# Gates before the convolved projections in an SSD and GLA layer, and decay triangles scaled four heads at a time

## The chip, the core and the metric

The kernel runs on one core of a Trainium2 chip. The metric is the device time of one execution in microseconds. The core's engines each run their own instruction queue and wait for one another by semaphores: TensorE (PE, matrix products; PEld is its weight load), VectorE (DVE), ScalarE (ACT), GpSimd (POOL) and SyncE (SP, here only the issue of weight transfers).

## The reference

The reference runs two blocks over 256 tokens of width 1024 and 256 context tokens. The first block has two layers, and the change lies in the second of them, "layer 1". Its mixer concatenates an SSD part and a GLA part, both scanned in both directions over the context and then the tokens. The modulation vectors (shift, scale and gate of the two norms) are products of the conditioning with a large matrix. Cut to what matters:

```python
z, xbc, dt_f, dt_b = split(p)                 # SSD
xbc = silu(dwconv_centred(xbc, conv_w, conv_b))
xs, bm, cm = split(xbc)                       # 512 + 256 + 256 channels
# scan in chunks of 128: decay = exp(segment sums of la), for 8 heads and both directions
y = rmsnorm((yf + yb + xs * d_skip) * silu(z)) # per group
# GLA: q, k, v, gate g; decayed scan in chunks, 4 heads
o = rmsnorm(scan(q, k, v)) * silu(g)
out = concat(y, o) @ w_out
```

Everything is computed in 32-bit precision.

## The kernel before

Weights arrive in tiles of 128x1024 numbers (512 KB) through SyncE's queue, strictly in the order in which the code asks for them, into a ring of four buffers (tile `w`, L32). A projection of 128 output channels, `gemm`, uses one tile: in halves of 512 columns it is split into a high part (ScalarE cast, L45) and a low part (VectorE subtraction, L46), and each of eight blocks is multiplied in three passes (L223, L224, L225) with the activations, whose parts are named `h0h`, `h0l` to `h7h`, `h7l`. One segment of activations is 256 columns. A projection of the tokens alone is therefore 24 matmuls, one of context and tokens is 48.

In `layer1` the small projections, q, k and v come first. Then the generator `gla` (L1007 on) is started: per chunk it makes decays, the intra-chunk products by levels (L1055 to L1081, L1078 being the last level's product for a chunk) and the states (L1099 to L1112); its last part makes the outputs from states and intra-chunk weights (L1132, L1133), their inverse norms on ScalarE (L186 and L195, after the sums of L209) and scales by them (L1135). The code then asks for the eight convolved projections xs, bm and cm: a copy out of PSUM (ScalarE L849), one tap on ScalarE (L851) and four multiply-adds on VectorE (L853), then silu by a tanh (L1213) and a VectorE operation (L1215). Inside the loop, behind projection 0, stand all the modulation steps that remain, two groups of 16 weight tiles; a group multiplies each tile with four matmuls (L154), copies and transposes the result (L161). After the convs ScalarE loads another table of functions (L177; logarithm and exponential), the rest of `gla` is taken, and then come the eight projections of the gates: z of SSD and gs of GLA, four each, halved into SBUF by L1233.

`ssd` (L906 on) follows: transposes of xs and bm (L918, L930) into the tile `sc`, products with the step sizes (L924, L927, `xd` and `xw`), a copy `bt` (L932), the chunk states (L936). For each of two chunks, two directions and two groups of four heads, the mask `TRI` is scaled by each head's log decay (L975, tile `lt`), multiplied by two constant matrices (L978, L980), put through the exponential (L981, L982; tiles `MT` and `CE`), and multiplied by the scores on GpSimd (L983) and by cm on VectorE (L984); the outputs are L992, L993 and L995. Then comes the output projection `w_out`, half of which needs only GLA's outputs (`o4` to `o7`) and is free to run earlier, and the memory stage (L1244 on).

The order of instructions on an engine is chosen by a scheduler from its own costs when the kernel is built, within the dependencies, and is fixed at run time. So an engine that waits for its next instruction runs none of the later ones.

Of the kernel before, what the change touches and what calls it, by code (L numbers as in the profile page):

```python
# [14 lines left out]
ALU = mybir.AluOpType  # L15
AX = mybir.AxisListType
PSUM = bass.MemoryType.PSUM
P = 128
# [58 lines left out]
class Kern:  # L77
# [827 lines left out]
    def ssd(self, pool, xs, bm, cm, z, d4, la, wend, etot, c1, out):  # L905
        nc = self.nc  # L906
# [52 lines left out]
        for c in range(2):  # L959
            ps = self.psum("sc")  # L960
            for gr in range(2):
                nc.tensor.matmul(ps[:, 128 * gr : 128 * gr + 128], lhsT=bm[gr][:, 256 + 128 * c : 384 + 128 * c],
                                 rhs=cm[gr][:, 128 * c : 128 * c + 128], start=True, stop=True)
            pair = []
            for d in range(2):
                cb = g("cb", (P, 2, 128), 2)
                nc.vector.tensor_tensor(cb, ps[:, 0:256].rearrange("p (g i) -> p g i", g=2),
                                        TRI[d].unsqueeze(1).broadcast_to([P, 2, 128]), op=ALU.mult)
                MT, CE = g("MT", (P, 8, 128), 2), g("CE", (P, 8, 128), 2)
                pair.append((MT, CE))  # L970
                for gr in range(2):
                    hs = slice(4 * gr, 4 * gr + 4)
                    lt = g("lt", (P, 4, 128), 2)
                    for h in range(4):
                        nc.vector.tensor_scalar(lt[:, h, :], TRI[d], la[:, 2 + c, 8 * d + 4 * gr + h : 8 * d + 4 * gr + h + 1], None, op0=ALU.mult)  # L975
                    l2 = lt.rearrange("p h i -> p (h i)")
                    p1 = self.psum("sc")
                    nc.tensor.matmul(p1, lhsT=ST[d], rhs=l2, start=True, stop=True)  # L978
                    p2 = self.psum("sc")
                    nc.tensor.matmul(p2, lhsT=self.C("ones"), rhs=l2, start=True, stop=True)  # L980
                    nc.scalar.activation(MT[:, hs, :], p1.rearrange("p (h i) -> p h i", h=4), AF.Exp)  # L981
                    nc.scalar.activation(CE[:, hs, :], p2.rearrange("p (h i) -> p h i", h=4), AF.Exp)  # L982
                    nc.gpsimd.tensor_tensor(MT[:, hs, :], MT[:, hs, :], cb[:, gr, :].unsqueeze(1).broadcast_to([P, 4, 128]), op=ALU.mult)  # L983
                    nc.vector.tensor_tensor(CE[:, hs, :], CE[:, hs, :],  # L984
                                            cm[gr][:, 128 * c : 128 * c + 128].unsqueeze(1).broadcast_to([P, 4, 128]), op=ALU.mult)
            for q in range(4):
                po = self.psum("po")
                for h in range(2):
                    o = po[64 * h : 64 * h + 64, 0:128]
                    hh = 2 * q + h  # L990
                    for d in range(2):
                        nc.tensor.matmul(o, lhsT=xd[d][c][:, hh, :], rhs=pair[d][0][:, hh, :], start=(d == 0), stop=False)  # L992
                        nc.tensor.matmul(o, lhsT=H[d][c][:, hh, :], rhs=pair[d][1][:, hh, :], start=False, stop=(d == 1))  # L993
                cs = slice(128 * c, 128 * c + 128)
                nc.vector.scalar_tensor_tensor(yt[q][:, cs], xs[q][:, 256 + 128 * c : 384 + 128 * c], self.V("d_skip")[:, q : q + 1], po[:, 0:128],  # L995
                                               op0=ALU.mult, op1=ALU.add)
# [140 lines left out]
    def layer1(self, xc, xl, sm, hm, HL):  # L1137
# [78 lines left out]
            return i  # L1216

        tanh, mods = [], (x for i in (1, 2) for x in self.mod_steps(1, i, cp, "mm"))
        for i in range(8):
            t = (xs + bm + cm)[i]  # L1220
            self.conv(cp, self.gemm(st, 72 + 8 * i, *(h if i < 6 else h[1:])), i, t, cw, cb)
            if i == 0:
                for _ in mods:
                    pass
            tanh.append(silu(t, last))
        for _ in mods:
            pass
        self.table(tanh)
        for _ in gla:
            pass  # L1230
        last = self.last
        for i in range(8):
            nc.scalar.mul((z + gs)[i], self.gemm(st, 136 + 8 * i, h[1]), 0.5)  # L1233
        M.close()
        G.close()
        H.close()
# [430 lines left out]
def blocks(w):  # L1667

    w = np.asarray(w)
    k, n = w.shape  # L1670
    return w.reshape(k // P, P, n // P, P).transpose(1, 2, 0, 3).reshape(P, -1, P)


def wide(w):

    w = np.asarray(w)
    return w.reshape(-1, P, w.shape[1]).transpose(1, 0, 2).reshape(P, -1, P)


def stream(*parts):  # L1680
    s = np.concatenate(parts, axis=1).reshape(P, -1)
    assert s.shape[1] % 2048 == 0, s.shape
    return np.ascontiguousarray(s.reshape(P, -1, 2048).transpose(1, 0, 2))
# [16 lines left out]
def prep(inp):  # L1700
# [46 lines left out]
    for l in range(2):  # L1747
# [7 lines left out]
    small = np.zeros((1024, P), np.float32)  # L1755
    small[:, 0:16], small[:, 32:48] = C[:, 1536:], D[:, 1536:]
    xbc = C[:, 512:1536]
    d["w_in1"] = stream(blocks(small), blocks(D[:, 256:512]), blocks(D[:, 0:256]), wide(D[:, 512:1024]), blocks(xbc), blocks(C[:, :512]),
                        blocks(D[:, 1024:1536]), np.zeros((P, 8, P), np.float32))
    up = np.zeros((P, 512), np.float32)  # L1760
    up[32:48, :256], up[32:48, 256:] = f["l1_gk_up_f"], f["l1_gk_up_b"]
    d["gk_up"] = up
# [59 lines left out]
```

## Time and profile before

| | us |
|---|---|
| median of 3 runs | 2034.68 (2032.78 to 2048.92) |
| profiled execution | 2034.45 |
| its span | 2032.7 |
| PE busy | 1910.7 (94%) |
| DVE busy | 1415.6 (70%) |
| ACT busy | 1160.0 (57%) |
| POOL busy | 277.4 (14%) |

The mean granted clock of TensorE is 0.974 of full speed. The part of layer 1 that the change touches lies between about 990 and 1190 us. The profile gives, by time, the busy share of each engine in a stretch, the chain of work that ended last, and each instruction with its start, length and the idle time before it. L12 is line 12 of the kernel; a tile is named out<-in.

### The profile page before, as it was taken

The numbers are of one execution on the slowest core, as the hardware profiler recorded it, in microseconds if no ns is written. First come the engines' busy times: TensorE is split into PE (matmuls) and PEld (weight loads), VectorE is DVE, ScalarE is ACT, GpSimd is POOL, SyncE is SP. The second block draws the span as 40 slices with busy tenths as digits, with TensorE's granted clock in tenths as the row PEclk, the third lists the DMA queues.
The fourth block names the chain that finished last, engine by engine and source line by source line (L and its number), as shares of the span: only waits on it lengthen the run. The fifth ranks groups of instructions, "written<-read, shape, count | busy, mean of one in ns | idle before, by whom it ended". The sixth has DMA issues, their size and how long they took to land.

```text
span 2032.7 us, 42311 instructions
## 1 busy us (share of the span) xinstructions
PE 1910.7 (94%) x16330; PEld 1725.6 (85%) x16330; DVE 1415.6 (70%) x2962; ACT 1160.0 (57%) x2527; POOL 277.4 (14%) x407
## 2 busy tenths in 40 slices
PE   5999999889999999999979999999999999989997
PEld 2886678669889998899739789999889998889997
DVE  3775966579767685567588977567776656677664
ACT  3655653465545675566546668476565555465553
POOL 1521110230100000001230210000012201012210
PEclk8999999889999999999989999999999999999999
DMA  8542430625116565765376435666325554325553
GB/s 307 167 138 70 166 125 22 218 85 157 42 45 190 185 195 185 237 216 175 115 243 187 135 115 178 187 186 189 103 86 184 182 183 137 103 84 165 183 183 114
DMA packets 91785, 313.26 MB, mean 154 GB/s; under 512 B 10304, under 2 KB 17728, under 8 KB 91584
## 3 DMA queue, kind: packets, MB, share of 16 engines
q1 hardware_dynamic: 83376, 299.94, 46.2%
q10 hardware_dynamic: 8208, 10.63, 1.7%
q8 instruction: 128, 2.10, 0.4%
q14 instruction: 73, 0.60, 0.1%
HBM read 309.48 MB, written 1.05 MB: 153 GB/s over the span
## 4 chain that ended last, share of the span: by engine, by line
PE 75%; DVE 10%; DMA 5%; ACT 4%; issue 2%; POOL 2%; POOLq 0%; ACTq 0%; SPq 0%; DVEq 0%
PE mm L224 16%; PE mm L223 16%; PE mm L225 16%; PE po L224 3%; PE po L225 3%; PE po L223 3%; DMA w<-in_mod 2%; PE mm L154 2%; DVE lo L46 1%; PE sc L532 1%; PE po L1383 1%; DMA w<-in_w_in 1%; DMA w<-in_mlp 1%; ACT hi L45 1%; DVE yy L1539 1%
## 5 line engine op out<-in xcount | busy, mean ns | idle before, releaser
L46 DVE TENSOR_TENSOR lo<-w,hi 128x512 fp32r<-128x512 f32 x948 | 651.5, 694 | 277.8 <-ACT hi L45 258.4
L45 ACT CAST hi<-w 128x512 fp32r<-128x512 f32 x948 | 576.5, 618 | 424.7 <-PE mm L224 290.0
L223 PE MATMUL mm<-u_h,hi 128*128 128x256 f32 x1120 | 318.9, 285 | 5.1 <-ACT u_h L216 5.0
L224 PE MATMUL mm<-u_l,hi 128*128 128x256 f32 x1120 | 317.2, 283 | 0.6 <-DVE u_l L217 0.4
L225 PE MATMUL mm<-u_h,lo 128*128 128x256 f32 x1120 | 317.6, 284 | 0.0
L223 PEld LDWEIGHTS mm<-u_h,hi 128*128 128x128 f32 x1120 | 214.0, 191 | 8.0 <-ACT u_h L216 5.6
L224 PEld LDWEIGHTS mm<-u_l,hi 128*128 128x128 f32 x1120 | 214.4, 192 | 1.2 <-DVE u_l L217 1.2
L225 PEld LDWEIGHTS mm<-u_h,lo 128*128 128x128 f32 x1120 | 214.0, 191 | 0.1
L154 PE MATMUL mm<-w,cs 128*32 128x256 f32 x640 | 68.1, 451 | 30.2 <-DMA w<-in_mod 29.9
L1588 POOL TENSOR_TENSOR ut<-ut,gt 128x256 f32<-128x256 f32 x44 | 53.9, 1226 | 200.1 <-ACT hi L45 170.5
L256 POOL TENSOR_SCALAR hf<-hf,g,mT 128x256 f32<-128x256 f32 x24 | 18.7, 781 | 413.5 <-ACT h1h L255 311.3
L154 PEld LDWEIGHTS mm<-w,cs 128*32 128x32 f32 x640 | 18.7, 118 | 58.1 <-DMA w<-in_mod 33.4
L217 DVE TENSOR_TENSOR u_l<-relu,u_h 128x256 fp32r<-128x256 f32 x96 | 40.7, 425 | 28.2 <-ACT u_h L216 28.0
L347 POOL TENSOR_SCALAR sht<-shf,mu 128x256 f32<-128x256 f32 x28 | 38.2, 1365 | 106.5 <-ACT shf L345 106.5
L216 ACT CAST u_h<-ut 128x256 fp32r<-128x256 f32 x44 | 17.9, 406 | 57.9 <-POOL ut L1588 57.9
L217 DVE TENSOR_TENSOR u_l<-ut,u_h 128x256 fp32r<-128x256 f32 x44 | 18.7, 425 | 43.8 <-ACT u_h L216 43.8
L223 PE MATMUL mm<-h0h,hi 128*128 128x256 f32 x130 | 39.7, 309 | 7.2 <-ACT shf L345 3.6
L1540 POOL TENSOR_TENSOR xl<-xl,yy 128x256 f32<-128x256 f32 x16 | 14.2, 888 | 228.1 <-DVE yy L1539 228.1
L69 POOL TENSOR_TENSOR sq<-sq 128x256 f32<-128x256 f32 x24 | 21.1, 880 | 154.6 <-ACT sq L61 151.7
L824 ACT ACTIVATE relu<-relu 128x256 f32<-128x256 f32 x96 | 39.6, 416 | 3.8 <-DVE h7l L257 1.5
L225 PE MATMUL mm<-h0h,lo 128*128 128x256 f32 x130 | 38.6, 297 | 3.1 <-DVE lo L46 3.1
L216 ACT CAST u_h<-relu 128x256 fp32r<-128x256 f32 x96 | 38.6, 405 | 2.2
(1125 smaller groups left out, 6116.1 us busy)
## 6 DMA issues: line engine op xcount, KB each, us to landing
w<-in_mlp SPq DMA_DIRECT2D x192, 512.0 KB, 4.3
w<-in_w_in SPq DMA_DIRECT2D x102, 512.0 KB, 4.3
w<-in_mod SPq DMA_DIRECT2D x96, 512.0 KB, 5.4
w<-in_ffn_in SPq DMA_DIRECT2D x88, 512.0 KB, 3.9
w<-in_ffn_out SPq DMA_DIRECT2D x44, 512.0 KB, 4.5
w<-in_w_out SPq DMA_DIRECT2D x40, 512.0 KB, 3.8
w<-in_memkv SPq DMA_DIRECT2D x8, 512.0 KB, 3.9
xc<-in_ctxT ACTq DMA_DIRECT2D x16, 128.0 KB, 4.8
```

The source lines that it names most:

```text
L45: nc.scalar.copy(self.hi, w)
L46: nc.vector.tensor_tensor(self.lo, w, self.hi, op=ALU.subtract)
L69: self.eng.tensor_tensor(sq, sq, self.acc, op=ALU.add)
L154: nc.tensor.matmul(ps[32 * j : 32 * j + 32, o : o + 256], lhsT=self.cs[:, k, :], rhs=w[:, 256 * j : 256 * j + 256], start=(k == 0), stop=( ...
L216: nc.scalar.copy(hi, src)
L217: nc.vector.tensor_tensor(lo, src, hi, op=ALU.subtract)
L223: nc.tensor.matmul(out, lhsT=wh, rhs=xh, start=start, stop=False)
L224: nc.tensor.matmul(out, lhsT=wh, rhs=xl, start=False, stop=False)
L225: nc.tensor.matmul(out, lhsT=wl, rhs=xh, start=False, stop=stop)
L347: nc.gpsimd.tensor_scalar(t, f[:, 1:257], self.mu1[:, i : i + 1], None, op0=ALU.mult)
L824: nc.scalar.activation(r, r, AF.Square)
L1588: nc.gpsimd.tensor_tensor(w, w, t, op=ALU.mult)
```

## The change

Three edits. The loop of the gates stands ahead of the convolved projections and takes two modulation steps (four tiles of modulation weights) behind each projection; what modulation is left is taken behind that loop. The columns of the weight matrix are laid out in the new order on the host. In `ssd` the four scalings of a 128x128 mask become one multiplication of 128x512, with the mask and the decays broadcast.

```diff
--- before.py
+++ after.py
@@ -971,8 +971,8 @@
                 for gr in range(2):
                     hs = slice(4 * gr, 4 * gr + 4)
                     lt = g("lt", (P, 4, 128), 2)
-                    for h in range(4):
-                        nc.vector.tensor_scalar(lt[:, h, :], TRI[d], la[:, 2 + c, 8 * d + 4 * gr + h : 8 * d + 4 * gr + h + 1], None, op0=ALU.mult)
+                    nc.vector.tensor_tensor(lt, TRI[d].unsqueeze(1).broadcast_to([P, 4, 128]),
+                                            la[:, 2 + c, 8 * d + 4 * gr : 8 * d + 4 * gr + 4].unsqueeze(2).broadcast_to([P, 4, 128]), op=ALU.mult)
                     l2 = lt.rearrange("p h i -> p (h i)")
                     p1 = self.psum("sc")
                     nc.tensor.matmul(p1, lhsT=ST[d], rhs=l2, start=True, stop=True)
@@ -1216,21 +1216,21 @@
             return i
 
         tanh, mods = [], (x for i in (1, 2) for x in self.mod_steps(1, i, cp, "mm"))
+
+        for i in range(8):
+            nc.scalar.mul((z + gs)[i], self.gemm(st, 72 + 8 * i, h[1]), 0.5)
+            next(mods)
+            next(mods)
+        for _ in mods:
+            pass
         for i in range(8):
             t = (xs + bm + cm)[i]
-            self.conv(cp, self.gemm(st, 72 + 8 * i, *(h if i < 6 else h[1:])), i, t, cw, cb)
-            if i == 0:
-                for _ in mods:
-                    pass
+            self.conv(cp, self.gemm(st, 136 + 8 * i, *(h if i < 6 else h[1:])), i, t, cw, cb)
             tanh.append(silu(t, last))
-        for _ in mods:
-            pass
         self.table(tanh)
         for _ in gla:
             pass
         last = self.last
-        for i in range(8):
-            nc.scalar.mul((z + gs)[i], self.gemm(st, 136 + 8 * i, h[1]), 0.5)
         M.close()
         G.close()
         H.close()
@@ -1755,8 +1755,8 @@
     small = np.zeros((1024, P), np.float32)
     small[:, 0:16], small[:, 32:48] = C[:, 1536:], D[:, 1536:]
     xbc = C[:, 512:1536]
-    d["w_in1"] = stream(blocks(small), blocks(D[:, 256:512]), blocks(D[:, 0:256]), wide(D[:, 512:1024]), blocks(xbc), blocks(C[:, :512]),
-                        blocks(D[:, 1024:1536]), np.zeros((P, 8, P), np.float32))
+    d["w_in1"] = stream(blocks(small), blocks(D[:, 256:512]), blocks(D[:, 0:256]), wide(D[:, 512:1024]), blocks(C[:, :512]),
+                        blocks(D[:, 1024:1536]), blocks(xbc), np.zeros((P, 8, P), np.float32))
     up = np.zeros((P, 512), np.float32)
     up[32:48, :256], up[32:48, 256:] = f["l1_gk_up_f"], f["l1_gk_up_b"]
     d["gk_up"] = up
```

On TensorE the place of the last L1078 shows the first move. Before, modulation matmuls and GLA's outputs (L1132, L1133) follow the last L1078:

```order
L1078 MATMUL po<-ql_12502,kl_12503 64x64 x4
L154 MATMUL mm<-w,cs 32x256 x7
L1132 MATMUL po<-qe_12562,S_12725 128x128
L1132 MATMUL po<-qe_12563,S_12943 128x128
L1133 MATMUL po<-at_12474,v 128x128
L1132 MATMUL po<-qe_12562,S_12747 128x128
L1132 MATMUL po<-qe_12563,S_12921 128x128
L154 MATMUL mm<-w,cs 32x256 x4
```

Now a gate's matmuls end in front of it and a block of 16 modulation matmuls stands right behind:

```order
L1078 MATMUL po<-ql_12502,kl_12503 64x64
L224 MATMUL mm<-h7l,hi 128x256
L225 MATMUL mm<-h7h,lo 128x256
L154 MATMUL mm<-w,cs 32x256 x16
L1132 MATMUL po<-qe_12562,S_12725 128x128
L1132 MATMUL po<-qe_12563,S_12943 128x128
L1133 MATMUL po<-at_12474,v 128x128
L1132 MATMUL po<-qe_12562,S_12747 128x128
```

What moved: ahead of this point stood 109 modulation matmuls and the 48 of conv 0; now 64 and 118 matmuls of gates. 64 modulation matmuls and three gates stand behind.

On VectorE, the end of the convs before SSD: `cm` is the last convolved tile, `xc` are GLA's outputs being scaled, `lo` the low part of a weight half. Before:

```order
L1135 SCALAR_TENSOR_TENSOR xc_4418<-po,c_vecs,rstd 128x256
L46 TENSOR_TENSOR lo<-w,hi 128x512 x2
L1135 SCALAR_TENSOR_TENSOR xc_4419<-po,c_vecs,rstd 128x256
L46 TENSOR_TENSOR lo<-w,hi 128x512
L1135 SCALAR_TENSOR_TENSOR xc_4420<-po,c_vecs,rstd 128x256
L46 TENSOR_TENSOR lo<-w,hi 128x512
L1135 SCALAR_TENSOR_TENSOR xc_4421<-po,c_vecs,rstd 128x256
L975 TENSOR_SCALAR lt<-c_cst_9116,la 128x128 x8
L1215 SCALAR_TENSOR_TENSOR z_9126<-th,z_9126 128x256
```

And now:

```order
L1215 SCALAR_TENSOR_TENSOR cm_9125<-th,cm_9125 128x256
L1135 SCALAR_TENSOR_TENSOR xc_4418<-po,c_vecs,rstd 128x256
L1135 SCALAR_TENSOR_TENSOR xc_4419<-po,c_vecs,rstd 128x256
L1135 SCALAR_TENSOR_TENSOR xc_4420<-po,c_vecs,rstd 128x256
L1135 SCALAR_TENSOR_TENSOR xc_4421<-po,c_vecs,rstd 128x256
L927 TENSOR_TENSOR xw<-sc,wend 128x512 x2
L974 TENSOR_TENSOR lt<-c_cst_9116,la 128x512 x2
L1215 SCALAR_TENSOR_TENSOR z_9126<-th,z_9126 128x256
```

What moved: the low parts of the gates' weights between the scalings have gone, the first eight lt scalings became two operations, and SSD's first xw products stand ahead of them.

On TensorE at the start of SSD (`o4h` and so on are GLA's outputs in the output projection). Before, the matmuls in front of the transposes L918 are the last gate's:

```order
L225 MATMUL mm<-h7h,lo 128x256
L918 MATMUL sc<-c_cst_87,xs_9118 128x128
L918 MATMUL sc<-c_cst_87,xs_9119 128x128
L918 MATMUL sc<-c_cst_87,xs_9120 128x128
L918 MATMUL sc<-c_cst_87,xs_9121 128x128
L930 MATMUL sc<-c_cst_87,bm_9122 128x128
L930 MATMUL sc<-c_cst_87,bm_9123 128x128
L223 MATMUL mm<-o4h,hi 128x256
L224 MATMUL mm<-o4l,hi 128x256
L225 MATMUL mm<-o4h,lo 128x256
```

And now they are those of the last conv, with the last two sums for GLA's norms (L209) between:

```order
L225 MATMUL mm<-h7h,lo 128x256
L209 MATMUL sc<-sq,c_cst_87 128x256 x2
L918 MATMUL sc<-c_cst_87,xs_9118 128x128
L918 MATMUL sc<-c_cst_87,xs_9119 128x128
L918 MATMUL sc<-c_cst_87,xs_9120 128x128
L918 MATMUL sc<-c_cst_87,xs_9121 128x128
L930 MATMUL sc<-c_cst_87,bm_9122 128x128
L930 MATMUL sc<-c_cst_87,bm_9123 128x128
L936 MATMUL sc<-xw,bt 128x256 x4
```

What moved: the last L209 stand between the convs and SSD, and the output projection's matmuls are no longer between SSD's transposes and its states. Between the first L918 and SSD's own L209, 59 of the 96 matmuls of GLA's half of the output projection stood before, and 9 stand now.

## Rows read from the trace of the kernel before

**Rows 1.** stretches of the span, busy us (instructions) by engine, granted clock, DMA.

```profile
core 0: us, PE busy (x) PEld busy (x) DVE busy (x) ACT busy (x) POOL busy (x), PEclk, DMA share, GB/s
...
993.00:1074.00 81.00, 67.99 (x867) 37.44 (x865) 69.20 (x162) 45.15 (x131) 26.87 (x48) 0.89 0.61 208
...
1065.20:1137.00 71.80, 71.71 (x587) 66.59 (x585) 61.47 (x119) 50.14 (x102) 2.26 (x12) 1.00 0.62 193
...
1137.00:1184.00 47.00, 40.70 (x265) 28.02 (x265) 42.23 (x86) 24.11 (x48) 17.91 (x15) 1.00 0.20 62
```

**Rows 2.** TensorE's instructions from 993 to 1065.3, grouped; last column idle time before.

```profile
L154 PE MATMUL mm<-w,cs 128*32 128x256 f32 x222 | 25.4, 429 | 9.6 <-DMA w<-in_mod 9.5
```

**Rows 3.** the chain of waits: start us, length us, engine, tile, line.

```profile
1064.78 0.44 PE po L1078 x8
...
1072.20 0.57 PE mm L154 x8
...
1073.40 0.64 PE po L1132 x4
...
1076.11 0.42 PE po L1133 x2
...
1117.79 1.28 ACT L177
...
1139.50 1.12 PE sc L936 x4
```

**Rows 4.** VectorE in order: start us, us, engine, line, operation, out<-in.

```profile
1022.50 0.74 DVE L853 SCALAR_TENSOR_TENSOR xs<-cvf,conv_w,xs 128x512 f32<-128x512 f32 x1
...
1074.97 1.28 DVE L46 TENSOR_TENSOR lo<-w,hi 128x512 fp32r<-128x512 f32 x2
```

**Rows 5.** DMA issues from 990 to 1215: count, KB each, us to landing.

```profile
w<-in_mod SPq DMA_DIRECT2D x29, 512.0 KB, 5.0
...
w<-in_w_in SPq DMA_DIRECT2D x20, 512.0 KB, 4.3
```

**Rows 6.** ScalarE in order, same columns, from the convs to SSD.

```profile
1094.26 0.58 ACT L849 COPY cvf<-mm 128x512 f32<-128x512 f32 x1
...
1099.88 0.58 ACT L849 COPY cvf<-mm 128x512 f32<-128x512 f32 x1
...
1112.00 0.35 ACT L849 COPY cvf<-mm 128x256 f32<-128x256 f32 x1
...
1124.28 0.47 ACT L186 ACTIVATE rstd<-sc,c_cst 128x256 f32<-128x256 f32 x1
...
1125.22 1.28 ACT L1213 ACT_TABLE_LOAD   x1
...
1126.51 0.42 ACT L1213 ACTIVATE th<-z 128x256 f32<-128x256 f32 x1
...
1138.86 0.35 ACT L932 COPY bt<-sc 128x256 f32<-128x256 f32 x1
```

**Rows 7.** two stretches of 2 us, TensorE only: busy, granted clock, DMA share.

```profile
1054.00:1056.00 2.00, 0.00 (x0) 0.76 0.89 311
...
1056.00:1058.00 2.00, 1.52 (x27) 0.50 1.01 397
```

**Rows 8.** VectorE in SSD, 1156 to 1186: lt grouped; then single rows.

```profile
L975 DVE TENSOR_SCALAR lt<-c_cst,la 128x128 f32<-128x128 f32 x24 | 11.8, 542 | 1.0 <-PE sc L980 1.0
...
1158.69 0.68 DVE L984 TENSOR_TENSOR CE<-CE,cm 128x512 f32<-128x512 f32 x1
...
1159.29 1.28 DVE L975 TENSOR_SCALAR lt<-c_cst,la 128x128 f32<-128x128 f32 x1
...
1181.01 1.00 DVE L984 TENSOR_TENSOR CE<-CE,cm 128x512 f32<-128x512 f32 x1 [1.57 <-ACT CE L982]
...
1185.21 0.33 DVE L995 SCALAR_TENSOR_TENSOR y<-xs,c_vecs,po 128x128 f32<-128x128 f32 x1
```

**Rows 9.** GpSimd in SSD, the MT product beside the slow lt.

```profile
1158.84 1.65 POOL L983 TENSOR_TENSOR MT<-MT,cb 128x512 f32<-128x512 f32 x1 [0.55 <-ACT MT L981]
```

More of the change, by code (lines that the diff above doesn't have):

```diff
@@ L1219, in layer1 @@
         for i in range(8):
-            t = (xs + bm + cm)[i]
-            self.conv(cp, self.gemm(st, 72 + 8 * i, *(h if i < 6 else h[1:])), i, t, cw, cb)
-            if i == 0:
-                for _ in mods:
-                    pass
-            tanh.append(silu(t, last))
+            nc.scalar.mul((z + gs)[i], self.gemm(st, 72 + 8 * i, h[1]), 0.5)
+            next(mods)
+            next(mods)
         for _ in mods:
             pass
+        for i in range(8):
+            t = (xs + bm + cm)[i]
+            self.conv(cp, self.gemm(st, 136 + 8 * i, *(h if i < 6 else h[1:])), i, t, cw, cb)
+            tanh.append(silu(t, last))
         self.table(tanh)
```

## The prediction

> **What bounds the kernel now.** I began with the busy times of stretches around the change [rows 1]. From 993 us, when the GLA chunks begin, to 1074 us TensorE is busy 67.99 of 81.00 us. From 1065.20 to 1137.00 us it is busy 71.71 of 71.80: there is no slack at all, so each matmul moved into or out of that stretch moves its end. In the SSD stretch from 1137 to 1184 VectorE is busiest (42.23 of 47.00 us) and TensorE has holes. The matmuls by group, up to the last intra-chunk matmul of GLA (L1078), then tell why the first stretch has holes: 9.5 us of idle time in front of the modulation's matmuls (L154), ended by the loads of their weights [rows 2]. The chain of waits gives the anchors [rows 3]: L1078 ends at 1064.78 + 0.44 = 1065.2; the table load on ScalarE at 1117.79; the first state matmul of SSD (L936) at 1139.50. The last y of SSD is written at 1185.21 [rows 8], and I take 1185.5 for its end. All sums are against the profiled execution, 2034.45 us, which is 0.01% under the median of 2034.68; so a shift against one is a shift against the other. About 1% (20.3 us: below 2014.3, above 2055.0) is what a measurement can tell from no change.
>
> The instruction order, not the diff, tells what moves. Before, 109 of the 128 modulation matmuls and conv 0 (48 matmuls) stood ahead of the last L1078 on TensorE; the 192 gates' matmuls stood behind the convs, ahead of SSD's first transposes. Now 64 modulation matmuls and 118 gates' matmuls (four z, the first gs nearly whole) stand ahead of that L1078. Behind it come the other 64 modulation matmuls in four blocks, three gates, GLA's outputs (L1132 and L1133, 32 and 16 as executed), all eight convs (336), and then SSD with no projection in front.
>
> **Step 1, up to the last L1078.** VectorE loses conv 0's four multiply-adds and its silu there (about 0.74 us each by the multiply-add's row, 3.7 us) and gains eight splits of gates' weights (L46, 0.60 to 0.64 us each, 4.8 to 5.1) [rows 4]: about +1. TensorE's work changes little: -45 modulation matmuls, 0.57 us to a load's four [rows 3] (about 6.4 us), -48 conv matmuls, +118 gates' matmuls at the pace below, +70 × 0.117 = 8.2; its slack holds +1.8. The 9.5 us in front of L154 should shrink, as 16 loads are queued there where 27 were; some of it becomes waits for gates' weights. I take 2.8 of it as gained: L1078 ends at 1065.2 + 1.1 - 2.8 = **1063.5**. Bounds: the VectorE cost with an equal new wait (+3), or twice that gain (-4).
>
> **Step 2, from there to the last conv matmul.** The pace of projections: the copies behind two convs of 48 matmuls start at 1094.26 and 1099.88 [rows 6], so 5.62 / 48 = 0.117 us each. Work on TensorE: 16 loads × 0.57 = 9.1; GLA's outputs in eight packs of 0.64 + 0.42 = 1.06 [rows 3], 8.5; three gates × 24 × 0.117 = 8.4; convs 336 × 0.117 = 39.4; transposes and sums 1.3. Together 66.8 us. To it come waits. SyncE's queue now alternates four modulation loads and one gate's, and the ring has four tiles. So the gate's load starts when the first modulation tile is used (0.6), lands 4.3 to 5.0 us later [rows 5], is split (0.6 and 0.6) and multiplied (2.8): about 9.1 us a cycle, for 5.1 us of matmuls. That is 4 us a cycle, unless GLA's outputs stand in the hole. In the order four packs of outputs (4.2 us) stand behind each of the first two blocks of modulation and nothing behind the last two; so two cycles cost up to 8 us, of which I take 6, since a tile may land sooner when few are in flight (bounds 0, if the loads run ahead during the GLA chunks, and 9). The last conv matmul: 1063.5 + 66.8 + 6 = **1136.3**.
>
> **Step 3, from there to SSD's first L936.** Before, the gates' matmuls filled TensorE while ScalarE finished the conv, loaded a table, made GLA's four inverse norms, loaded the other table and began z's tanh. In the order that chain now stands bare: SSD's transposes (L918) follow the last conv and two sums (L209), VectorE has the four scalings by the norms (L1135) ahead of SSD's first product (L927), and ScalarE has z's tanh ahead of the copy of bt (L932). From the last conv copy to the table load it took 5.8 us (1112.00 [rows 6] to 1117.79 [rows 3]) with gates' casts between; without them I take 5.0. Then a table load 1.28; four norms at 0.94 (1124.28 to 1125.22), 3.8; a table load 1.28; tanh and copy 0.31 + 0.35 [rows 6]. Sum 12.0 (bounds 11, if VectorE's tail is the later one and shorter, and 14, with 2 us of hand-overs that the sum leaves out). L936 starts at **1148.3**, against 1139.5: **+8.8**.
>
> **Step 4, SSD.** Its 24 small lt scalings in this stretch take 11.8 us, mean 542 ns; alone one takes 0.27, but one took 1.28 [rows 8] when GpSimd's MT product ran beside it (1158.84 to 1160.49) [rows 9]. Eight more were done ahead of it. Now there are eight merged ones, all behind the start. The trace has no such operation. The nearest are the CE products, 128x512 on the same engine with a broadcast operand: 0.68 free and 1.00 when GpSimd ran beside it [rows 8]. Two merged ones take the place of the early eight and stand where TensorE's states hold the chain; the other six cost 3.6 to 6.0 us. That saves 5.8 to 8.2 us on VectorE, of which I take 5, because VectorE is not alone on that path: the exponentials and GpSimd's products stand on it too. Bounds -2 and -9. The stretch goes from 46 to **41 us**.
> The Trainium skill, page "SBUF — State Buffer", section "Who interferes with whom", speaks against the merge: VectorE and GpSimd share a pair of ports under an exclusive lock; a product with both inputs in SBUF contends with a GpSimd operation that reads SBUF, as a two-port scalar operation does, and the one that issues first blocks the other. By that the merged form is no freer of GpSimd than the small ones; the 1.00 us CE agrees in direction, and what it would make of the time is the rival R4.
>
> **Step 5, behind SSD.** In the order 59 of the 96 matmuls of GLA's half of the output projection stood inside SSD, in the holes of TensorE [rows 1]; now 9 do. The 50 others go behind: 50 × 0.117 = 5.9, less about 1 that fills idle time there: **+5** (4 to 6). GpSimd's queue only loses the memsets' place, ScalarE's casts of gates swap with those of convs, and the reordered w_in columns are the same bytes; these cost nothing as long as the casts stay 0.2 us ahead of TensorE.
>
> Sum: +8.8 - 5 + 5 = +8.8, so 2034.45 + 8.8 = **2043 us**. Its own range is 2036 to 2050: step 2's wait at 0 to 9 (-6, +3) and step 4's two ends together are not all reached at once.
>
> **Rivals.**
> R1, loads run ahead. If SyncE's queue gets through its cycles beside the GLA chunks, conv 0 starts before about 1091 and there is no wait: last conv matmul near 1127.8, L936 at 1139.8 (+0.3), SSD at its better end (-8), +4.5 behind: 2034.45 - 3.2 = 2031 (2026 to 2036). For it: the ring was starved only in part before, and DMA is busy 0.61 in that stretch [rows 1]. Against it: four tiles and a 4.3 us landing time [rows 5]. Chance 0.22.
> R2, the bare tail is dearer, slower than before. Its place is between the last conv matmul and L936, its price is idle TensorE; it decides once that gap passes 13 us and the waits of step 2 reach 9 together. Before, 2 us without a matmul were followed by a granted clock of 0.50, the 1.2 GHz level of the two, in the next 2 us [rows 7]; a 13 us gap would bring the same at SSD's start, where I price it at +3 from that row and its neighbours. The sum: +3 waits, +1 tail, +3 clock, SSD only -2, +6 behind, which is 2034.45 + 8.8 + 3 + 1 + 3 + 3 + 1 = 2054 (2050 to 2060). Chance 0.13.
> The Trainium skill, page "TensorE: Matmul & The Clock Gate", Part 1, ties the clock to how busy the engine has been; the half level behind the idle stretch agrees [rows 7].
> R3, the gates fill every hole of the GLA stretch. TensorE is idle 13.0 us of 81 there, and its granted clock of 0.89 over 81 us costs another 8.9 of full-speed work [rows 1]; together 21.9 us, nearly the 192 × 0.117 = 22.5 of all gates. If the gates took both, the last conv matmul would come 0.6 later than now, near 1112.6, L936 12.0 later at 1124.6 (-14.9), and with SSD's -5 and the +5 behind it the time is 2019.5 (2012 to 2026). The order speaks against it, since three gates stay behind the last L1078, and [rows 2] has only 9.5 us of the idle time that other loads end. Chance 0.07.
> R4, the merged product is blocked by GpSimd each time: six at 1.28 plus GpSimd's remainder, so step 4 gives only -0.6 in place of -5: 2047.7. Against it: CE products beside MT took 1.00 at most. Chance 0.06.
> The forecast keeps 0.52.
>
> **How the numbers follow.** The time is the forecast's, 2043. A range from 2026 to 2053 takes in the forecast's own range, R1 and R4, and half of R2; it leaves out R3, the rest of R2 and the far ends of the others, under 0.2 together. Faster by over 1% is the part of R3 below 2014.3, and a little of the unforeseen: 0.03. Slower by over 1% is the part of R2 above 2055: 0.06. Within 1%: 0.91.
>
> **What would show it.** The last L1078 near 1063 and the last conv copy near 1136; between them waits of modulation and gate matmuls for w. No matmul of a projection between the last conv and SSD, and a gap of some 10 us in which ScalarE loads two tables. Merged lt of 0.6 to 1.0 us, last y about 1189 to 1190. Output projection matmuls behind y. I am wrong if conv 0 starts before 1091, if a merged lt takes over 1.2 us, or if the gap before L936 is under 8 us.

## The result, and the profile after

The changed kernel takes 2061.13 us (median of 4 runs, 2052.89 to 2067.16) against 2035.46 for the kernel before: ratio 1.0114, 95% interval 1.0077 to 1.0150. It is slower by 1.1%; the prediction said 2043, within 1% of before, with a range to 2053. The execution that was profiled took 2065.51 us, one of the two longer ones, 31.06 more than the profiled one of before; 2.2 of these lie ahead of the change, so times below are counted from each trace's first GLA gate product (L1024: 992.5 before, 994.8 after).

| step | predicted | measured | miss |
|---|---|---|---|
| 1: last L1078 | -1.7 | +1.5 | +3.2 |
| 2: from its end to the last conv copy | 72.8 | 80.7 | +7.9 |
| 3: from there to the first L936 | 12.0 | 14.0 | +2.0 |
| 4: SSD, to the end of the last y | 41 | 48.1 | +7.1 |
| 5: more behind SSD, to the memory's L1314 | +5 | +5.2 | +0.2 |

The misses sum to 20.4, and 8.8 + 20.4 = 29.2 us is the loss up to L1314, counted from L1024. The stretches of the changed kernel, in the columns of [rows 1]:

```profile
core 0: us, PE busy (x) PEld busy (x) DVE busy (x) ACT busy (x) POOL busy (x), PEclk, DMA share, GB/s
996.00:1069.00 73.00, 61.80 (x775) 40.71 (x773) 63.56 (x149) 43.39 (x128) 27.97 (x46) 0.86 0.44 145
1069.00:1112.00 43.00, 35.87 (x301) 28.10 (x302) 14.52 (x33) 11.82 (x26) 0.00 (x0) 0.92 0.77 256
1112.00:1150.00 38.00, 35.14 (x295) 34.57 (x294) 35.03 (x57) 27.73 (x47) 0.80 (x12) 1.00 0.55 168
1150.00:1163.50 13.50, 4.24 (x10) 2.00 (x10) 7.91 (x18) 8.15 (x16) 0.00 (x0) 0.50 0.25 80
1163.50:1212.00 48.50, 40.57 (x222) 25.16 (x222) 41.06 (x70) 23.96 (x53) 20.82 (x19) 0.93 0.07 22
```

Where TensorE had no slack for 71.80 us before [rows 1], it now idles 7.1 us among the last gates and the modulation's blocks (43.00 - 35.87), 2.9 beside the convs, and 9.3 of the 13.5 in front of SSD, where the granted clock is 0.50, the 1.2 GHz level. SSD runs at 0.93 where it had 1.00.

In the first stretch the loads' waits did go, as step 1 said: 9.5 us in front of L154 [rows 2] are 1.5. But other waits grew, L1075's for VectorE and GpSimd to 6.1 us from 2.1, so TensorE's idle time from the first L1024 to the last L1078 only fell from 13.0 to 11.2 us; its busy time rose from 59.7 to 63.0, and the stretch did not get shorter. One of TensorE's groups up to the last L1078 before, and two after:

```profile
L1075 PE MATMUL po<-ql,kl 64*64 64x64 f32 x384 | 12.4, 246 | 2.1 <-POOL ql L1061 1.0 <-DVE kl L1062 0.8
...
L1075 PE MATMUL po<-ql,kl 64*64 64x64 f32 x384 | 15.0, 253 | 6.1 <-DVE kl L1062 4.4 <-POOL ql L1061 1.4 <-DVE cend L1095 0.2
L154 PE MATMUL mm<-w,cs 128*32 128x256 f32 x128 | 14.2, 455 | 1.5 <-DMA w<-in_mod 1.5
```

Behind it, TensorE in order (idle time and its releaser at the end):

```profile
1088.77 1.93 PE L154 MATMUL mm<-w,cs 128*32 128x256 f32 x32
1094.22 0.38 PE L223 MATMUL mm<-h0h,hi 128*128 128x256 f32 x1 [3.52 <-ACT hi L45]
...
1097.05 0.41 PE L223 MATMUL mm<-h4h,hi 128*128 128x256 f32 x1
...
1099.26 1.93 PE L154 MATMUL mm<-w,cs 128*32 128x256 f32 x32
...
1105.01 0.39 PE L223 MATMUL mm<-h0h,hi 128*128 128x256 f32 x1 [2.46 <-ACT hi L45]
```

A cycle of four modulation tiles and a gate takes 10.5 us (1088.77 to 1099.26); the prediction's 9.1 had the same kind of wait. What it left out stands in the third row: a matmul behind the wait takes 0.41 us where it takes 0.28 at the full clock.

The tail, ScalarE in order:

```profile
1149.65 0.35 ACT L849 COPY cvf<-mm 128x256 f32<-128x256 f32 x1
...
1154.42 0.42 ACT L1213 ACTIVATE th<-cm 128x256 f32<-128x256 f32 x1 [2.89 <-DVE cm L853]
1154.85 1.28 ACT L177 ACT_TABLE_LOAD   x1
...
1157.62 0.47 ACT L186 ACTIVATE rstd<-sc,c_cst 128x256 f32<-128x256 f32 x1 [0.55 <-DVE xc L1135]
...
1161.63 1.28 ACT L1213 ACT_TABLE_LOAD   x1
1162.92 0.42 ACT L1213 ACTIVATE th<-z 128x256 f32<-128x256 f32 x1
1163.24 0.35 ACT L932 COPY bt<-sc 128x256 f32<-128x256 f32 x1
```

It is the chain of [rows 6], bare: the table load stands 5.2 us behind the last conv copy (predicted 5.0), and the four norms then take 5.5 us up to the next table load (predicted 3.8), because each further norm waits for VectorE's scaling of the one before it (0.55 us in the row shown). VectorE inside SSD:

```profile
1178.39 0.41 DVE L1215 SCALAR_TENSOR_TENSOR gs<-th,gs 128x256 f32<-128x256 f32 x1
...
1182.20 0.94 DVE L217 TENSOR_TENSOR o5l<-xc,o5h 128x256 fp32r<-128x256 f32 x1
1183.07 1.48 DVE L1283 TENSOR_TENSOR sq<-sq 128x256 f32<-128x256 f32 x1
1184.47 0.68 DVE L974 TENSOR_TENSOR lt<-c_cst,la 128x512 f32<-128x512 f32 x1
...
1189.29 1.49 DVE L217 TENSOR_TENSOR o7l<-xc,o7h 128x256 fp32r<-128x256 f32 x1
...
1202.67 1.76 DVE L974 TENSOR_TENSOR lt<-c_cst,la 128x512 f32<-128x512 f32 x1
```

and GpSimd beside it:

```profile
1182.02 0.84 POOL L1244 TENSOR_TENSOR xc<-xc,gs 128x256 f32<-128x256 f32 x1 [0.87 <-DVE gs L1215]
1182.83 1.43 POOL L983 TENSOR_TENSOR MT<-MT,cb 128x512 f32<-128x512 f32 x1
```

A free merged lt takes 0.68 us, as the CE of [rows 8] did. The silu of z and gs, the products with gs on GpSimd (L1244) and the low parts of GLA's outputs (L217) now stand behind SSD's first L936: eight L1215, four L1244 and four L217, where one, one and two stood there before. The long instructions shown (1.48, 1.49, 1.76) overlap products of GpSimd; that these lengthen them is inferred from the overlap.

### The profile page after: what moved, and what is told of

Same layout as the page of the kernel before. It is cut to its first block, busy times and chain, and to the rows that moved or that the text cites. A ratio compares the mean times of both kernels' runs of the same rounds, so it can differ in the third digit from the quotient of the medians.

```text
span 2063.7 us, 42280 instructions
## 1 busy us (share of the span) xinstructions
PE 1921.3 (93%) x16330; PEld 1734.4 (84%) x16330; DVE 1414.9 (69%) x2938; ACT 1160.8 (56%) x2527; POOL 277.7 (13%) x407
## 3 DMA queue, kind: packets, MB, share of 16 engines
q1 hardware_dynamic: 83376, 299.94, 45.4%
## 4 chain that ended last, share of the span: by engine, by line
PE 74%; DVE 12%; ACT 5%; DMA 4%; issue 3%; POOL 2%; ACTq 0%; POOLq 0%; DVEq 0%; SPq 0%
PE mm L223 16%; PE mm L224 16%; PE mm L225 16%; PE po L224 3%; PE po L225 3%; PE po L223 3%; DVE lo L46 2%; DMA w<-in_w_in 2%; PE sc L532 1%; PE mm L154 1%; PE po L1383 1%; DMA w<-in_mod 1%; ACT hi L45 1%; DMA w<-in_mlp 1%; DVE yy L1539 1%
## 5 line engine op out<-in xcount | busy, mean ns | idle before, releaser
L154 PE MATMUL mm<-w,cs 128*32 128x256 f32 x640 | 62.3, 450 | 21.1 <-ACT cs L136 10.4
L256 POOL TENSOR_SCALAR hf<-hf,g,mT 128x256 f32<-128x256 f32 x24 | 18.9, 786 | 417.5 <-ACT h1h L255 310.2
L217 DVE TENSOR_TENSOR u_l<-relu,u_h 128x256 fp32r<-128x256 f32 x96 | 40.7, 426 | 28.2 <-ACT u_h L216 28.1
L154 PEld LDWEIGHTS mm<-w,cs 128*32 128x32 f32 x640 | 19.4, 119 | 46.9 <-DMA w<-in_mod 21.0
L223 PE MATMUL mm<-h0h,hi 128*128 128x256 f32 x130 | 40.4, 314 | 13.5 <-ACT hi L45 7.0
L217 DVE TENSOR_TENSOR u_l<-ut,u_h 128x256 fp32r<-128x256 f32 x44 | 18.7, 425 | 43.8 <-ACT u_h L216 43.8
L223 PEld LDWEIGHTS mm<-h0h,hi 128*128 128x128 f32 x130 | 24.7, 191 | 24.8 <-ACT hi L45 8.7
```

Of the source, the lines that this page charges most:

```text
L154: nc.tensor.matmul(ps[32 * j : 32 * j + 32, o : o + 256], lhsT=self.cs[:, k, :], rhs=w[:, 256 * j : 256 * j + 256], start=(k == 0), stop=( ...
L217: nc.vector.tensor_tensor(lo, src, hi, op=ALU.subtract)
L223: nc.tensor.matmul(out, lhsT=wh, rhs=xh, start=start, stop=False)
```

## The experiments

Each ran five rounds or more beside the kernel before on the same chip, where that had medians of 2034.79 to 2036.34; ratios are against that. The last six columns are us of one profiled execution each: its whole time, two starts counted from the first L1024, and three lengths. Where that execution is far from the median (e12, e16, e17), the lengths are to be read with care.

| kernel | median us | ratio (95%) | profiled us | last L1078 | last conv copy | gap to L936 | SSD to the last y's start | to L1314 |
|---|---|---|---|---|---|---|---|---|
| before | 2035.46 |  | 2034.45 | 72.5 | 119.5 | 27.5 | 45.7 | 18.6 |
| changed | 2061.13 | 1.0114 (1.0077, 1.0150) | 2065.51 | 74.0 | 154.9 | 14.0 | 47.8 | 23.9 |
| e1 merge only | 2036.77 | 1.0009 (0.9995, 1.0022) | 2035.75 | 73.7 | 121.1 | 27.6 | 44.3 | 18.7 |
| e2 order only | 2070.41 | 1.0169 (1.0149, 1.0190) | 2070.69 | 74.1 | 155.0 | 14.0 | 51.9 | 24.2 |
| e3 modulation at convs | 2067.78 | 1.0168 (1.0149, 1.0187) | 2067.78 | 75.0 | 162.3 | 15.7 | 48.2 | 24.1 |
| e5 silu early | 2053.35 | 1.0090 (1.0067, 1.0112) | 2055.99 | 74.4 | 154.8 | 13.5 | 45.8 | 19.5 |
| e4 gs behind | 2053.22 | 1.0087 (1.0056, 1.0118) | 2053.86 | 73.2 | 143.1 | 16.6 | 47.1 | 23.9 |
| e6 modulation at gate 0 | 2050.28 | 1.0067 (1.0047, 1.0088) | 2050.03 | 69.4 | 141.1 | 14.0 | 47.7 | 23.9 |
| e9 one split | 2057.78 | 1.0095 (1.0068, 1.0123) | 2056.19 | 74.0 | 153.4 | 13.8 | 47.7 | 23.7 |
| e12 z ahead, gs behind | 2046.88 | 1.0038 (1.0008, 1.0068) | 2056.32 | 74.8 | 138.0 | 16.1 | 48.4 | 22.4 |
| e10 norms early | 2046.69 | 1.0042 (1.0021, 1.0064) | 2048.61 | 79.1 | 160.3 | 2.0 | 46.0 | 22.1 |
| e13 norms, modulation | 2039.77 | 1.0007 (0.9982, 1.0032) | 2043.42 | 68.2 | 145.6 | 1.9 | 49.3 | 20.9 |
| e14 norms, mod., split | 2037.00 | 0.9996 (0.9974, 1.0018) | 2038.94 | 70.3 | 147.6 | 1.9 | 45.8 | 18.9 |
| e15 conv 0 first | 2054.43 | 1.0076 (1.0051, 1.0101) | 2054.93 | 73.1 | 157.0 | 1.9 | 46.3 | 23.5 |
| e16 conv 0, silu late | 2050.12 | 1.0066 (1.0044, 1.0088) | 2036.54 | 74.3 | 151.9 | 1.9 | 52.2 | 20.7 |
| e17 conv 0, split | 2043.70 | 1.0041 (1.0019, 1.0062) | 2037.92 | 79.4 | 154.4 | 1.9 | 49.1 | 18.7 |
| e18 before, merge, split | 2038.97 | 1.0001 (0.9982, 1.0020) | 2040.67 | 77.6 | 124.0 | 28.3 | 44.3 | 18.7 |

**e1 and e2: the halves of the change.** Against the kernel before, and against the changed one:

```diff
 # e1, against before
-for h in range(4): nc.vector.tensor_scalar(lt[:, h, :], TRI[d], la[...], None, op0=ALU.mult)
+nc.vector.tensor_tensor(lt, TRI[d]..broadcast.., la..broadcast.., op=ALU.mult)
 # e2, against the changed kernel: the same lines the other way
```

> The kernel before with the merged lt product alone; the order of the projections stays. Theory P (the time is lost by the places: waits for loads between the gates, a bare tail in front of SSD, SSD crowded by what stood ahead of it): 2031 to 2036 us, as the merge saves 4 to 5 us of VectorE's time in SSD and part of it is lost to the other operations there. Rival M (the merged product costs, since GpSimd blocks it): 2042 us or more.

> The changed kernel with the four small lt scalings put back; only the order of projections and modulation differs from the kernel before. Theory P: 2058 to 2068 us, all of the loss is here. Rival M: under 2050 us.

The merge costs nothing that these runs can tell: rival M falls, though e1's time is 0.8 us above theory P's range too. The whole loss is the order's, 1.69%, a little more than theory P's upper end; the merge gives 4.1 us of SSD back in that order (51.9 to 47.8) and 1.4 in the order of before, where the time shows no gain. SSD in the kernel before and in e2, in the columns of [rows 1]:

```profile
1139.50:1185.20 45.70, 39.97 (x262) 27.64 (x262) 40.62 (x83) 22.35 (x43) 17.81 (x15) 1.00 0.18 55
1165.80:1217.70 51.90, 43.05 (x220) 26.14 (x220) 40.39 (x93) 23.39 (x51) 20.05 (x18) 0.87 0.06 20
```

By the order alone SSD is 6.2 us longer, though VectorE has no more to do in it. TensorE runs 42 instructions fewer (filling of the output projection) and is yet busy 3.1 us longer, at a granted clock of 0.87 for 1.00; the other 3.1 us are idle time.

**e3: modulation at the convs.**

```diff
-    next(mods); next(mods)            # behind each gate
+    next(mods); next(mods)            # behind each conv
```

> The changed kernel with two modulation steps behind each conv in place of each gate. Convs of 48 matmuls take 5.6 us, so a conv's load should land beside the one before. If the waits for loads between the gates and the half clock behind them are the larger part (theory P, its waits): 2044 to 2052 us, with conv 0 begun some 14 us sooner than in the changed kernel and some 9 us of modulation matmuls now between convs. If the bare tail and the crowded SSD are the larger part (theory P, its tail): 2055 to 2062 us.

Neither: it is dearer still. The convs did not hide the loads. TensorE's groups from 1065 to 1153 in e3:

```profile
L223 PE MATMUL mm<-h0h,hi 128*128 128x256 f32 x13 | 4.4, 337 | 15.2 <-ACT hi L45 14.9 <-ACT cvf L849 0.3
```

14.9 us of waiting for a conv's split weights, which stand behind four modulation tiles in the queue. And with hardly any modulation in front the last L1078 came no sooner (75.0).

**e5: the gates' silu ahead of the convs.**

```diff
+    tanh += [silu(t, last) for t in z + gs]     # behind the gates
-    self.table([silu(t, last) for t in z + gs]) # inside SSD
```

> The changed kernel with the silu of z and gs ahead of the convs, where the gates are ready; the two table loads behind GLA's norms go, and so do eight tanh and eight VectorE operations from SSD. If SSD is longer because of what was moved into it (theory P, its tail): SSD from the first L936 to the last y 44 us or less in place of 48, the gap in front of it 12 us or less in place of 13.9, and 2046 to 2054 us. If SSD's length has another cause (the clock, or GpSimd's locks of the merged product): SSD stays at 47 us or more and the time is 2057 us or more.

The time meets theory P, the lengths less so: the gap hardly moved (13.5), SSD gave 2.0 (45.8, where 44 or less was asked), and 4.4 came from behind SSD: 44 matmuls of GLA's half of the output projection stand inside SSD again, where the changed kernel has 9 and the kernel before 52 (from the first L936 to the last y).

**e4: the gs gates behind the convs.**

```diff
-    for i in range(8): <gate i>; next(mods); next(mods)
+    for i in range(4): <gate i>; next(mods); next(mods)
...
+    for i in range(4, 8): <gate i>
```

> The changed kernel with the four gs gates put back behind the convs; the z gates and their modulation steps stay ahead. If the bare tail is a loss of its own (theory P): the gs gates, 96 x 0.117 = 11.2 us of matmuls that now stand elsewhere, fill most of the 13.9 us between the last conv copy and the first L936, TensorE idles there under 4 us and keeps the full clock; the second half of the modulation then stands in a row, which costs its waits as before. 2045 to 2053 us. If the tail does not matter, because the same matmuls only change places: 2058 us or more.

The time is just above the expected range (2053.22). TensorE is busy 12.40 us in the gap, where the changed kernel had 4.24 of 13.5, and the gap is only 2.6 longer; the clock in it is 0.95. With the gs gates gone from ahead of the convs, the first L936 comes 9.2 us sooner:

```profile
1137.00:1153.40 16.40, 12.40 (x92) 11.30 (x92) 12.81 (x25) 13.04 (x27) 0.00 (x0) 0.95 0.60 193
```

**e6: all modulation behind the first gate.**

```diff
     <gate i>
-    next(mods); next(mods)
+    if i == 0:
+        for _ in mods: pass
```

> The changed kernel with all modulation behind the first gate, the place that it had behind conv 0; the gates still stand ahead of the convs. Theory L (the modulation's loads need the GLA stretch, where TensorE waits for other engines anyway; taken out of it, they cost waits between the gates and a half clock behind them): the stretch up to the last L1078 stays at 73 to 75 us from the first L1024, the waits between gates go, and the last conv copy comes at 142 to 147 us instead of 154.9; 2048 to 2055 us. If the GLA stretch grows with what is put into it: last L1078 at 78 us or later, and 2058 us or more.

The time is in theory L's range, and the last conv copy comes 13.8 us sooner, at 141.1, a little below its range; 4.6 of these lie ahead of the last L1078 (69.4), which L had expected to stay. The stretch behind GLA's chunks is full again, as it was before [rows 1], and the GLA stretch is not longer:

```profile
core 0: us, PE busy (x) PEld busy (x) DVE busy (x) ACT busy (x) POOL busy (x), PEclk, DMA share, GB/s
996.00:1066.00 70.00, 57.63 (x791) 30.72 (x792) 58.45 (x141) 39.04 (x118) 26.44 (x46) 0.85 0.62 210
1066.00:1101.00 35.00, 35.00 (x287) 31.82 (x279) 20.95 (x43) 17.57 (x37) 0.00 (x0) 1.00 0.61 206
```

**e9: one split for both segments of a conv.**

```diff
-    self.mm3(ps[:, o : o + T], st.cols((b0 + k) * 128, 128), x, ...)
+    if not keep or o == 0: kept.append(st.cols((b0 + k) * 128, 128))
+    self.mm3(ps[:, o : o + T], kept[k] if keep else kept[-1], x, ...)
```

> The changed kernel, in which the second segment of a conv uses the split weights of the first, so that each conv of 48 matmuls loads and splits its tile once and not twice: 12 casts and 12 subtractions and 6 loads fewer, no matmul fewer. If the convs are bound by VectorE once they stand alone (theory D: 5.9 us of VectorE's work for 5.6 us of matmuls): the last conv copy 3 us or more sooner, and 2054 to 2058 us. If they are bound by TensorE: no change beyond 2 us, 2059 to 2063.

The time lies in theory D's range, but the last conv copy came only 1.5 us sooner, half of what D asked; the intervals of e9 and the changed kernel overlap. So VectorE's bound is at most a small part; the first four convs of the changed kernel also follow each other at 5.63 us, TensorE's pace in [rows 6].

**e12: a version from these readings.**

```diff
-for i in range(8): <gate i>; next(mods); next(mods)
+for i in range(4): <gate i>; for _ in range(4): next(mods)
+tanh += [silu(t, last) for t in z]
...
+for i in range(4): <gs gate i>
...
-    self.table([silu(t, last) for t in z + gs])
+    self.table([silu(t, last) for t in gs])
```

> A version drawn from the readings: the z gates ahead with four modulation steps behind each (so all modulation stays in the GLA stretch), z's silu ahead of the convs, the gs gates behind the convs as cover of the tail, and the merged lt. Theory P with L: last L1078 at 73 to 76 us from the first L1024, no waits between gates, the first L936 at 144 to 149, SSD 42 to 45 us, and 2026 to 2034 us. If the GLA stretch cannot take three gates beside the loads: 2038 us or more.

The time, 2046.88, is the rival's, 2038 or more. The last L1078 is where it was foretold, but L936 comes at 154.0 and SSD takes 48.4, and the GLA stretch took no more of TensorE's work than before: with three z gates in it, conv 0 and part of the modulation are out of it. The profiled execution is the slowest of the twelve, with a granted clock of 0.80 in that stretch, so its times are no average.

**e10, e13, e14: the chain taken out of the tail.**

```diff
 # e10, against the changed kernel
+for _ in gla: pass                     # outputs and norms ahead of the convs
+last = self.last
+tanh += [silu(t, last) for t in z + gs]
 <convs, each with its silu>
 self.table(tanh)
-for _ in gla: pass
-    self.table([silu(t, last) for t in z + gs]) # inside SSD
 # e13: and e6's edit.  e14: and e9's edit.
```

> The changed kernel with GLA's outputs, their norms and the silu of z and gs taken ahead of the convs; nothing else moves. Theory C (the gates behind the convs covered a chain: table load, four norms, table load, the gates' silu and products, which also made GLA's half of the output projection ready as filling for SSD; with the cover gone the chain stands bare in front of SSD and inside it): from the last conv copy to the first L936 under 7 us instead of 13.9, SSD 46 us or less with the output projection's matmuls back in it, and 2042 to 2050 us. If the chain was not the cause: the gap stays over 10 us and the time over 2054.

> The kernel with norms and silu ahead of the convs, and all modulation behind the first gate. If C and L (loads of the modulation belong into the GLA stretch) are two losses that add: another 8 to 12 us less than without the second move, 2032 to 2040 us. If they overlap: 2042 us or more.

> As the one before it, and the second segment of a conv uses the split weights of the first. Theory D (convs that stand alone are bound by VectorE): another 3 to 5 us less, 2028 to 2036 us, the last conv copy 36 us or less behind the first gate-free start of the convs. If VectorE is not what binds them now: no change beyond 1 us.

The chain is shown for the gap: without it the first L936 starts 2.0 us behind the last conv copy, and gap, SSD (46.0) and time are where theory C had them. The output projection came back into SSD only in part, with 19 matmuls. ScalarE in e10, where the copy bt no longer waits for a table:

```profile
1149.08 0.35 ACT L849 COPY cvf<-mm 128x256 f32<-128x256 f32 x1
1149.53 0.60 ACT L851 ACTIVATE cm<-cvf,conv_b,conv_w 128x256 f32<-128x256 f32 x1
1150.67 0.37 ACT L932 COPY bt<-sc 128x256 f32<-128x256 f32 x1 [0.54 <-PE sc L930]
```

Theory L's move takes another 6.9 us (expected 8 to 12); its time is in the range. The split takes 2.8 more (expected 3 to 5), within the noise, and e14's 2037.00 is above its range; from the first conv copy to the last it takes 38.5 us, as e13's 38.4, so the trace shows nothing of theory D. e14 is level with the kernel before: its gates stand ahead of the convs, and nothing of the loss is left. Its SSD is as short as that of the kernel before, at full clock:

```profile
1144.10:1190.00 45.90, 39.57 (x253) 26.75 (x253) 40.05 (x64) 17.06 (x31) 16.77 (x14) 1.00 0.14 47
```

But the chain's absence does not by itself make SSD short: it takes 49.3 in e13, which differs from e14 by the split alone and has 5.3 us more of VectorE's work in it (low parts of GLA's outputs and the memory stage; 45.4 us busy for 40.1).

**e15, e16, e17: conv 0 first.**

```diff
 # e15: conv 0 with its silu, all modulation, the gates, norms, silu, convs 1 to 7
 # e16: conv 0's silu behind the norms
-silu(xs[0], last)                      # ahead of the norms
+tanh += [silu(t, last) for t in z + gs + xs[:1]]
 # e17: and e9's edit
```

> Conv 0 and all modulation in their places of the kernel before, then the gates, GLA's outputs and norms, the gates' silu, then convs 1 to 7; merged lt. The gates still stand ahead of all convs but one. If the loss came from what the gates' early place did to the loads and to the chain behind the convs, and not from the early place itself: 2028 to 2038 us, the same as the kernel before within 0.3%, or a little faster.

> As the version with conv 0 and the modulation first, but conv 0's tanh is taken behind GLA's norms; one edit. In that version conv 0's tanh stands ahead of the norms, and its trace shows eight table loads of 1.28 us in the norms (one ahead of each logarithm and each exponential) and TensorE idle from 1100 to 1130. If that is why it stayed at 2054 (theory T): no table load between the norms, the last conv copy 8 us or more sooner (149 or less from the first L1024), and 2034 to 2044 us. If conv 0's early place itself costs: 2050 us or more.

> As the one before it, and a conv's second segment uses the split weights of the first. With conv 0's work on VectorE done in the GLA stretch and 12 splits gone, the convs should be bound by TensorE alone: the last conv copy 3 us or more sooner, and 2028 to 2037 us. If the convs are no longer bound by VectorE: within 1.5 us of the one before it.

All three missed their main range; e16's 2050.12 is its rival's, 2050 or more. e16's edit took the table loads out of the norms, and the last conv copy came 5.1 us sooner, where theory T asked 8. There was less to gain than it said: in e15 TensorE is not idle from 1100 to 1130, it is busy 24.5 of these 30 us. In e16 the convs run beside a VectorE that is full (27.51 of 28.00 us):

```profile
1106.00:1134.00 28.00, 24.97 (x195) 24.36 (x194) 27.51 (x43) 21.34 (x42) 3.94 (x12) 0.94 0.47 156
```

e17 then gained 6.4 us in the medians, though the intervals overlap and its last conv copy comes 2.6 us later, not 3 sooner. Why this order stays above e14 is left open. Up to L1314 the trace of e17 is 10.0 us behind that of e14: 9.1 at the last L1078, at a granted clock of 0.76 for 0.88, and 3.3 in SSD, at 0.90 for 1.00, less 2.3 between.

**e18: the split in the order before.**

```diff
 # against before: e1's edit and e9's edit
```

> The kernel before with the merged lt and with one split for both segments of a conv; the order of the projections stays as before. There the convs ran at 5.62 us for 48 matmuls, TensorE's own pace, and gates stood behind them. If VectorE binds the convs only where they stand alone (theory D): 2032 to 2037 us, no gain beyond 0.2%. If it also binds in the order before: 2030 us or less.

No gain, and 2038.97 is above the range given: the convs' copies follow each other at 5.66 to 5.79 us where the kernel before had 5.62 to 5.64, so VectorE did not bind them there. No version that ran beats the kernel before.

## Why the prediction was wrong

The sign of the sum was right, the size was not: +8.8 against +25.7 in the medians. All five misses have the same sign. Step 2 has the largest, a term that was mis-sized; step 4 is the step that failed, by what it left out. By the steps:

- **Step 1** took a shorter wait for a shorter stretch. The wait in front of L154 shrank by 8.0 us, but most of it came back as waits of L1075 and others, TensorE's own work grew by 3.3 us (1.8 predicted), and the end moved 1.5 the wrong way. What sets that end is not shown. e3, with hardly any modulation in the stretch, and e6, with nearly all, end it at 75.0 and 69.4; but e10, which has the changed kernel's instructions up to there, ends it at 79.1, at a granted clock of 0.78 for 0.86. So 1.5 us are within what two executions differ by.
- **Step 2** had the waits: 6 predicted, 7.1 us idle measured. It priced the work around them at the full clock and the convs without idle time. From 1069 to 1150 TensorE is busy 71.0 us for the 66.8 of the sum and idle 10.0 for 6. At 0.92 the 35.87 busy us of the first 43 hold some 2.9 more than at full clock (an estimate from these two numbers); 2.9 of the idle time lie beside the convs. e6 took the waits away and 13.8 us with them, 4.6 of these ahead of the last L1078.
- **Step 3** was right in mechanism (14.0 for 12.0, the upper bound given). The miss is the norms: 5.5 us for 3.8. The sum took four times the busy 0.94 and no hand-over, though from table load to table load they had taken 6.15 us before (1119.07 [rows 3] to 1125.22 [rows 6]). e10 shows that the chain of norms and tables is the gap.
- **Step 4** is the step that failed. "The stretch goes from 46 to 41 us" counted only what the diff does to SSD, and put at nothing what the order does to it. The merge gave 4.1 us in the new order (e2 against the changed kernel), near the 5 that were taken, but only 1.4 in the old: there three of its six lt are slow (1.30 to 1.75 us) and the six sum to 6.7, above the 3.6 to 6.0 predicted; in the changed kernel they sum to 5.8. The order alone lengthens SSD by 6.2 us (45.7 to 51.9 in e2). With the gates' cover went the filling of the output projection, and the gates' silu, L1244 and L217 now stand in SSD; I had seen z's tanh and left the rest uncounted. What is shown of the 6.2 is that half is longer busy time of TensorE, at 0.87 for 1.00, and half idle time, and that taking the silu out gives 2.0 back (e5). How the rest divides between the moved work, GpSimd's products and the clock is open: e16 and e17 have neither the chain nor the gates' silu in SSD, and it takes 52.2 and 49.1 there.
- **Step 5** was right, 5.2 for 5. That it comes from the same cover is shown by e5, which gave 4.4 of it back.
- **The rivals.** R2 is the one that came: a gap of 14.0, and 10.0 us idle in step 2. It named the bare tail and the clock behind it; its 2054 was too low because it let SSD shrink as well. R4's slow product is seen in two of six lt (1.31 and 1.76 us), and one CE (1.75) and sums (1.48) are as slow; but e1 shows the merge as a whole costing nothing. For such overlaps the Trainium skill, page "SBUF — State Buffer", section "Who interferes with whom", names a pair of ports that VectorE and GpSimd share, so that one blocks the other; each of these long rows stands beside a product of GpSimd. R1 and R3 did not occur. The deciding point of R1, conv 0 before 1091, was missed by 14 us (its first matmul is the row at 1105.01).

## What to carry to other kernels

Work that stands late on the critical engine may be the cover of a chain on the others: before moving it, list the whole chain behind the point, with what it makes ready for later, and not only the part that touches the next stage. Loads with little arithmetic (here 0.57 us of matmuls for 512 KB) belong where that engine waits for others anyway; moved between gates or convs they cost waits here, 7.1 us in the changed kernel and 14.9 in e3. A wait on TensorE is to be priced with the slower matmuls behind it (0.41 us for 0.28 here).

## What the runs showed of the hardware

The granted clock was 0.50 through the 13.5 us in front of SSD, in which TensorE was busy 4.24 us, and 0.93 in the 48.5 us behind. In e4, with gates in that gap, it is 0.95 in the gap and 0.94 in SSD, and the slow stretch has only moved. It starts behind the waits for the norms and for bt at the gap's end, and reaches into SSD, where TensorE is busy again:

```profile
core 0: us, PE busy (x), PEclk, DMA share, GB/s
1150.00:1152.00 2.00, 0.47 (x3) 0.96 0.67 227
1152.00:1154.00 2.00, 0.59 (x1) 0.50 0.47 156
1154.00:1156.00 2.00, 2.00 (x6) 0.50 0.41 133
1156.00:1158.00 2.00, 2.00 (x8) 0.50 0.00 0
```

In the changed kernel the clock is back at 1.00 from 1168, and at 0.50 once more from 1174 to 1176, behind 2 us in which TensorE was busy 0.55. So both the bare gap and SSD's own holes are followed by the lower level; no run gives the price of each.

Executions of one kernel differ more than I had expected, 2025.97 to 2056.32 us in e12, at mean clocks of 0.981 and 0.963. The same holds for a stretch: the changed kernel and e10 run the same instructions from the first L1024 to the last L1078, and take 74.2 us at a granted clock of 0.86 and 79.2 at 0.78.
